# The overfull-expert branch of a two-layer MoE trunk moves from the first expert pair to the last, and a 1 MB weight piece loads earlier

## The chip, the cores and the metric

The kernel runs on one core of one Trainium2 chip. The metric is the device time of one execution in microseconds (us). A core has five engines, each with an instruction queue of its own: TensorE (PE: matmuls, with weight loads shown as PEld), VectorE (DVE), ScalarE (ACT), GpSimdE (POOL) and SyncE (SP), which here issues nearly all DMA transfers. Engines wait for one another on semaphores, each of which is a counter.

## The reference

Two layers, each of a token mixer and a mixture of experts, on 256 tokens of width 1024. The change touches the experts:

```python
for l in range(DEPTH):
    ...
    x = x + g1 * token_mix(h, positions, w_in[l], ...)
    h = rmsnorm(x, norm2_g[l]) * (1.0 + sc2) + sh2
    x = x + g2 * grouped_moe(h, w_router, router_bias, w_gate[l], w_up[l], w_down[l])
return rmsnorm(x, final_g)

def grouped_moe(h, w_router, router_bias, w_gate, w_up, w_down):
    ...                                   # 2 of 16 experts per token, weights in combine
    for e in range(N_EXPERTS):
        he = jax.nn.silu(t @ w_gate[e]) * (t @ w_up[e])
        y = y + combine[:, e:e + 1] * (he @ w_down[e])
```

## The kernel before

Each layer is a mixer and then `moe`. The router gives each of 16 experts its tokens, and a matmul with one-hot matrices (`gather`) copies up to CAP = 64 tokens of an expert into `xe` (in the trace `o`). The experts run in 8 pairs, `p` = 0 to 7: a gate product (`pair_mm(xs, 0, p)`), an up product (`pair_mm(xs, 1, p)`), `he` = silu(gate) times up on DVE, four transposes of `he` on PE, their copy `heT` on ACT, and the down product (`down`), whose result is scaled by the router's weights (`take_out`) and added to `xT` through a scatter matmul (`scatter`). In the last pair the down product goes in four pieces, each followed by a scatter, and then come the squares (`square_sum`) for the next norm. `warm` loads ACT's function table for the coming square root ahead of its use.

More than 64 tokens can pick one expert. `overflow()` handles them: all five engines load the largest count, `cmaxi`, into a register (L1141) and compare it with CAP at `tc.If` (L1144). On these inputs no engine takes the block: each jumps over its code and raises its semaphores by what the block would have raised them (EVENT_SEMAPHORE rows of L1144). Matmuls after the block write PSUM banks that the block's code uses too, so their waits count the semaphores past it. In the kernel before, the block stands between the gather and the first pair.

SP issues the weight loads in an order fixed when the program is built. `fetch` puts one into a buffer known by a tag; `issue` goes through the list `todo` and takes what has a free buffer: expert pieces ("moe", layer, pair, matrix, half) and the next mixer's sections ("sec", layer, name, half), of which "lat" comes first. Before the experts start, the first pair's weights and part of the second's are loaded: `early` and `late` put pieces into buffers that the mixer has done with. The last 1 MB of the second pair's up weights goes into buffer `n8`, by `latest`, after the block, because the block uses `n8` for its own tile `hT`.

The list of a tile scheduler, not the source alone, sets where instructions of different parts stand on an engine. The next mixer's first weight section is split into a rounded part and a rest: four CASTs on ACT and four TENSOR_TENSORs on DVE (helper line L409, reading `sec_lat_0A`). They stand, before the change, between the last squares of layer 0.

Of the kernel before, what the change touches and what calls it, by code (L numbers as in the profile page):

```python
# [50 lines left out]
HALF = SEC // 2  # L51
QUART = SEC // 4
# [103 lines left out]
def trunk(ctx: ExitStack, tc: tile.TileContext, x, pos, vec_in, msk_in, lat_in, wb, wq_in, wkv_in, ada_in, adat_in, crow_in, we,  # L156
# [10 lines left out]
    def nm(s):  # L167
        uid[0] += 1
        return f"{s}_{uid[0]}"

    def bank():
        return ps.tile([P, 512], F32, tag="bank", name=nm("bank"))
# [12 lines left out]
    free = set(size) - {"vm", "attn", "hA"}  # L185
# [3 lines left out]
    def load(o, src):  # L189
        tc.keep_in_program_order(nc.sync.dma_start(o, src))  # L190

    def fetch(key, tag, src, at=0, cuts=1):
        assert tag in free, (key, tag)
        free.discard(tag)
        n = src.shape[-1]
        t = wk.tile([P, size[tag]], F32, tag=tag, bufs=1, name=nm("_".join(map(str, key)) + tag))
        o = t if len(src.shape) == 2 else t.rearrange("p (q n) -> p q n", n=n)
        for c in range(cuts):
            c = slice(c * n // cuts, (c + 1) * n // cuts)
            load(o[..., c], src[..., c])  # L200
        held.setdefault(key, []).append((at, t, tag))
# [20 lines left out]
    def first_load(h):  # L222
        for q in (h, h + 1):
            for i in (1, 0):
                nc.sync.dma_start(first[i, h][:, (q - h) * QUART:(q - h + 1) * QUART], ada_in[i, q])
# [10 lines left out]
    def issue():  # L236
        while todo and not todo[0]:
            todo.pop(0)
        for n, part in enumerate(todo[:2]):
            while part:  # L240
                key = part[0]
                if key[0] == "sec":
                    tags = ("A0", "A1", "B0") if key[2] in ("lat", "qf") else ("A0", "A1")
                elif key[1] > layer[0] or n and todo[0] and (todo[0][0][0] == "moe" or todo[0][0][2] in ("lat", "qf")):
                    break
                else:
                    tags = ("B0", "B1", "C0", "C1", "x0", "x1") + (() if n and todo[0] else ("A0", "A1"))
                s = [t for t in tags if t in free and t not in blocked]
                if not s:
                    break  # L250
                part.pop(0)
                if key[0] == "sec":
                    _, l, name, h = key
                    fetch(key, s[0], lat_in[l, h] if name == "lat" else wb[l, SECTIONS.index(name), h],
                          cuts=4 if key == ("sec", 1, "lat", 0) else 1)
                    if key == ("sec", 0, "lat", 0):
                        first_load(2)
                else:
                    _, l, p, i, h = key
                    fetch(key[:4], s[0], we[l, p, i][:, h * HALF:(h + 1) * HALF], h * HALF,  # L260
                          cuts=(1 if p < E // 2 - 1 else 4 if (i, h) in ((1, 1), (2, 1)) else 2))
            if part and part[0][0] == "moe":
                break
        while atodo:
            s = [t for t in ("r0", "r1") if t in free]
            if not s:
                break
            key = atodo.pop(0)
            fetch(key, s[0], adat_in[key[1:]])
# [6 lines left out]
            at += size[t]  # L276

    def late(l):
        free.add("hA")
        fetch(("moe", l, 1, 1), "hA", we[l, 1, 1][:, HALF:HALF + QUART], HALF)  # L280

    def latest(l):
        at = HALF + QUART
        fetch(("moe", l, 1, 1), "n8", we[l, 1, 1][:, at:at + QUART], at)

    def take(*key):
        return held[key][0][1]
# [2 lines left out]
        free.update(tag for _, _, tag in held.pop(key))  # L290
        issue()

    again, used_up = {}, {}

    def spent(l, p, i, j):
        for e in list(held["moe", l, p, i]):
# [642 lines left out]
    def moe(l):  # L939
# [187 lines left out]
        def scatter(p, chunks=range(4)):  # L1127
            for i in chunks:
                b = bank()
                for q in range(2):  # L1130
                    j = 2 * i + q
                    for n in range(2):
                        mm(b[:, q * T:(q + 1) * T], yv[:, n, j * P:(j + 1) * P], St[p // 4][:, p % 4, :],
                           n == 0, n == 1)
                for q in range(2):
                    j = 2 * i + q
                    ve.scalar_tensor_tensor(xT[:, j, :], b[:, q * T:(q + 1) * T], g2[:, j:j + 1],  # L1137
                                            xT[:, j, :], op0=ALU.mult, op1=ALU.add)

        def overflow():  # L1140
            over = nc.values_load(cmaxi[0:1, 0:1], engines=[ENG.SP, ENG.Activation, ENG.DVE, ENG.PE, ENG.Pool],  # L1141
                                  min_val=0, max_val=T)
            room = [t2("room", [P, 512]) for _ in range(4)]
            with tc.If(over > CAP):  # L1144
                hT = solo("n8", [P, J, T])
                for t in range(NT):
                    for i in range(2):
                        b = bank()
                        for q in range(4):
                            for n, x in enumerate((hth, htl)):  # L1150
                                mm(b[:, q * P:(q + 1) * P], x[:, t, 4 * i + q, :], identr, n == 0, n == 1)
                        for q in range(4):
                            j = 4 * i + q
                            ve.tensor_scalar(hT[:, j, t * P:(t + 1) * P], b[:, q * P:(q + 1) * P],
                                             acol[:, j:j + 1], sh2[:, j:j + 1], op0=ALU.mult, op1=ALU.add)
                with tc.For_i(0, E // 2, 1) as p:
                    for q in range(2):
                        spill(l, p, q, hT, left[:, :, q::2], g2, room)
# [1 line left out]
        gather(oh, (0, 1), 2)  # L1160
        gather(oh, (2, 3))
        weights(0, oh)
        overflow()
        latest(l)
        for p in range(E // 2):
            xs = lambda j, q: xe[:, j, p % 2, 64 * q:64 * q + 64]
            bg = pair_mm(xs, 0, p)
            he = t2("he", [P, FJ, P])
            sg = t2("sg", [P, FJ, P])
            ac.activation(sg, bg.rearrange("s (j f) -> s j f", j=FJ), AF.Silu)  # L1170
            last = p == E // 2 - 1
            if last:
                scatter(p - 1)
            nxt = p + 1 if p % 2 and not last else None
            if nxt:
                oh = one_hot(nxt)
            bu = pair_mm(xs, 1, p)
            ve.tensor_tensor(he, bu.rearrange("s (j f) -> s j f", j=FJ), sg, ALU.mult)  # L1178
            if nxt:
                gather(oh)  # L1180
                weights(nxt, oh)
                build_scatter(nxt, oh)
            elif p and not last:
                scatter(p - 1, (0, 1))
            b = bank()
            for j in range(FJ):
                pe.transpose(b[:, j * P:(j + 1) * P], he[:, j, :], ident)  # L1187
            heT = t2("heT", [P, FJ, P])
            ac.copy(heT, b.rearrange("p (j s) -> p j s", j=FJ))  # L1189
            if p and not last:  # L1190
                scatter(p - 1, range(4) if nxt else (2, 3))
            wc = wcol[:, p:p + 1]
            def take_out(b, c, n):
                d = slice(c * 256, (c + n) * 256)
                s = slice(c % 2 * 256, (c % 2 + n) * 256)
                ac.activation(yv[:, 0, d], b[:, s], AF.Copy, scale=wc)  # L1196
                ve.scalar_tensor_tensor(yv[:, 1, d], b[:, s], wc, yv[:, 0, d], op0=ALU.mult, op1=ALU.subtract)  # L1197

            if last:
                warm(heT[:, 0, 0:1])  # L1200
            else:
                b0, b1 = bank(), bank()
                down(heT, p, b0, 0, 2)
            if p == 0:
                down(heT, p, b1, 2, 1)
                down(heT, p, b1, 3, 1)
                St = [solo(n, [P, 4, T], F32R) for n in ("vm", "attn")]
                yv = solo("r1", [P, 2, D], F32R)
                build_scatter(0, one_hot(0))
                take_out(b0, 0, 2)  # L1210
                take_out(b1, 2, 2)
            elif not last:
                take_out(b0, 0, 2)
                down(heT, p, b1, 2, 2)
                take_out(b1, 2, 2)
            else:
                for c in range(4):
                    b = bank()
                    down(heT, p, b, c, 1)
                    take_out(b, c, 1)  # L1220
                    if c:
                        scatter(p, (c - 1,))
# [89 lines left out]
```

## Time and profile before

| | |
|---|---|
| median of 3 runs | 987.47 us (983.97 to 988.82) |
| the profiled execution | 983.23 us |
| its span, first to last instruction | 981.4 us |
| mean granted TensorE clock | 0.963 of full |
| PE busy | 893.2 us, 91% of the span |
| DMA | 316.71 MB, mean 323 GB/s |

The profiled execution is 4.2 us under the median. Layer 0's experts take about 293 to 510 us of the span, layer 1's about 755 to 972 us; in these stretches PE works nearly without a break and the DMA queues are close to full. A matmul row's time is modelled, so a busy PE is not PE at its peak.

### The profile page before, as it was taken

The page shows a single profiled execution, that of the slowest core. Times are in us where ns is not written, and L with a number is a line of the kernel's source. Part 1 is how long each engine was busy: PE and PEld are TensorE (multiplying, and loading weights), DVE is VectorE, ACT ScalarE, POOL GpSimd, SP SyncE. Part 2 cuts the span into 40 slices and gives each one's busy share as a digit, 9 for nine tenths or more (in the row PEclk, how much of TensorE's full clock was granted, in tenths as well). Part 3 has the DMA queues.
Part 4 walks back from the last instruction along what each step waited for, and adds up shares of the span by engine and source line. Part 5 has one row for each costly group of instructions (what it writes and reads, how often), then busy time and mean ns, then how long its engine had stood idle before and what let it go on. Part 6 is the DMA issues. An engine that isn't in the chain of part 4 may idle for free. (4 is left out here: it accounts for less than half of the span.)

```text
span 981.4 us, 14762 instructions
## 1 busy us (share of the span) xinstructions
PE 893.2 (91%) x5958; PEld 635.6 (65%) x5958; DVE 524.3 (53%) x972; ACT 340.5 (35%) x632; POOL 51.9 (5%) x42
## 2 busy tenths in 40 slices
PE   5899999967969999999979999997895999999995
PEld 3688999957953535344349989997894353535333
DVE  4469898998540322222256968979854122322224
ACT  5465564524340212111146646554434111111103
POOL 0001100023000000000000020002300000000002
PEclk9899999998879999999999999999997999999998
DMA  9996665977659899999978626686585979999991
GB/s 362 430 378 225 234 224 217 380 307 315 253 210 381 344 384 430 434 427 429 422 299 329 271 91 248 253 326 250 224 348 200 398 306 433 429 429 433 426 386 43
DMA packets 35648, 316.71 MB, mean 323 GB/s; under 512 B 3952, under 2 KB 4208, under 8 KB 13808
## 3 DMA queue, kind: packets, MB, share of 16 engines
q1 hardware_dynamic: 35568, 315.64, 79.5%
q8 instruction: 50, 0.82, 0.3%
q14 instruction: 30, 0.25, 0.1%
HBM read 314.58 MB, written 1.05 MB: 322 GB/s over the span
## 5 line engine op out<-in xcount | busy, mean ns | idle before, releaser
L551 PE MATMUL bank<-hA,x 128*128 128x256 f32 x1312 | 242.8, 286 | 16.1 <-ACT x L409 8.8
L551 PEld LDWEIGHTS bank<-hA,x 128*128 128x128 f32 x1312 | 205.5, 192 | 20.3 <-DVE x L409 9.9
L551 PE MATMUL bank<-hB,x 128*128 128x256 f32 x656 | 184.7, 282 | 0.0
L551 PEld LDWEIGHTS bank<-hB,x 128*128 128x128 f32 x656 | 125.9, 192 | 0.2
L1178 DVE TENSOR_TENSOR he<-bank,sg 128x512 f32<-128x512 f32 x16 | 11.1, 692 | 141.8 <-PE bank L1112 113.4
L1137 DVE SCALAR_TENSOR_TENSOR xT<-bank,mod,xT 128x256 f32<-128x256 f32 x128 | 52.9, 478 | 58.1 <-PE bank L181 58.1
L1197 DVE SCALAR_TENSOR_TENSOR r<-bank,small,r 128x512 fp32r<-128x512 f32 (+1 forms) x36 | 24.7, 691 | 95.1 <-ACT r L1196 95.1
L1196 ACT ACTIVATE r<-bank,small 128x512 fp32r<-128x512 f32 (+1 forms) x36 | 22.8, 638 | 103.4 <-PE bank L1121 103.2
L1112 PE MATMUL bank<-moe_0B,o 128*64 128x512 f32 x192 | 47.6, 645 | 6.0 <-DVEq L1144 3.4
L1170 ACT ACTIVATE sg<-bank 128x512 f32<-128x512 f32 x16 | 9.6, 597 | 111.6 <-PE bank L1112 111.6
L1112 PE MATMUL bank<-moe_1x,o 128*64 128x512 f32 x192 | 43.4, 593 | 0.0
L1103 ACT ACTIVATE o<-bank,mod,acol 128x256 f32<-128x256 f32 x32 | 18.1, 564 | 58.5 <-DVE o L1105 55.0
L1189 ACT COPY heT<-bank 128x512 f32<-128x512 f32 x16 | 9.4, 588 | 83.4 <-PE bank L1187 83.4
L1112 PEld LDWEIGHTS bank<-moe_0B,o 128*64 128x64 f32 x192 | 15.2, 148 | 33.1 <-issue 32.6
L1112 PE MATMUL bank<-moe_1C,o 128*64 128x512 f32 x160 | 36.1, 592 | 0.0
L1105 DVE TENSOR_SCALAR o<-bank,acol,mod 128x256 f32<-128x256 f32 x32 | 17.4, 544 | 31.1 <-PE bank L181 28.2
L551 PE MATMUL bank<-o,x 128*128 128x256 f32 x192 | 28.1, 304 | 6.4 <-ACT x L409 3.4
L551 PE MATMUL bank<-attn,x 128*128 128x256 f32 x128 | 26.6, 300 | 6.4 <-DVE x L409 5.0
L1121 PE MATMUL bank<-moe_2C,heT 128*64 128x512 f32 (+1 forms) x160 | 29.2, 511 | 2.7 <-ACT heT L1189 2.7
L697 POOL TENSOR_TENSOR x<-ra,rbt 32x512 f32<-32x512 f32 x8 | 12.9, 1613 | 354.0 <-DVE rbt L693 353.5
L551 PEld LDWEIGHTS bank<-o,x 128*128 128x128 f32 x192 | 26.4, 212 | 7.2 <-ACT x L409 3.8
L1112 PEld LDWEIGHTS bank<-moe_1x,o 128*64 128x64 f32 x192 | 13.9, 137 | 26.2 <-issue 25.9
(298 smaller groups left out, 1719.6 us busy)
## 6 DMA issues: line engine op xcount, KB each, us to landing
moe_0B<-in_we SPq DMA_DIRECT2D x8, 2048.0 KB, 9.5
moe_1x<-in_we SPq DMA_DIRECT2D x8, 2048.0 KB, 13.0
moe_0A<-in_we SPq DMA_DIRECT2D x8, 2048.0 KB, 12.5
moe_1C<-in_we SPq DMA_DIRECT2D x6, 2048.0 KB, 12.3
moe_2C<-in_we SPq DMA_DIRECT2D x6, 2048.0 KB, 14.0
moe_1A<-in_we SPq DMA_DIRECT2D x6, 2048.0 KB, 18.1
moe_2A<-in_we SPq DMA_DIRECT2D x6, 2048.0 KB, 15.4
moe_2x<-in_we SPq DMA_DIRECT2D x6, 2048.0 KB, 20.1
```

The lines of the kernel that those rows point to most:

```text
L551: pe.matmul(o, a[:, k, :], b[:, k0 + k, :], start=first and k == 0 and q == 0, stop=last and k == 3 and q == 2)
L697: gp.tensor_tensor(qT[64:96, i::4, :], ra[q4], rbt[q4], ALU.add)
L1103: ac.activation(o, bq, AF.Identity, bias=sh2[:, j:j + 1], scale=acol[:, j:j + 1])
L1105: ve.tensor_scalar(o, bq, acol[:, j:j + 1], sh2[:, j:j + 1], op0=ALU.mult, op1=ALU.add)
L1112: pe.matmul(b[64 * q:64 * q + 64, :], x(j, q), w[:, o:o + 512], start=(j == 0), stop=(j == J - 1), tile_position=(0, 64 * q))
L1121: pe.matmul(b[64 * q:64 * q + 64].rearrange("p (c n) -> p c n", n=256)[:, c % 2:c % 2 + n], x[:, j, 64 * q:64 * q + 64], _ap(w[:, o:o + 25 ...
L1137: ve.scalar_tensor_tensor(xT[:, j, :], b[:, q * T:(q + 1) * T], g2[:, j:j + 1], xT[:, j, :], op0=ALU.mult, op1=ALU.add)
L1170: ac.activation(sg, bg.rearrange("s (j f) -> s j f", j=FJ), AF.Silu)
L1178: ve.tensor_tensor(he, bu.rearrange("s (j f) -> s j f", j=FJ), sg, ALU.mult)
L1189: ac.copy(heT, b.rearrange("p (j s) -> p j s", j=FJ))
L1196: ac.activation(yv[:, 0, d], b[:, s], AF.Copy, scale=wc)
L1197: ve.scalar_tensor_tensor(yv[:, 1, d], b[:, s], wc, yv[:, 0, d], op0=ALU.mult, op1=ALU.subtract)
```

## The change

It does four things in each of the two layers. `overflow()` leaves the place ahead of the first pair and stands in the last pair, behind the copy `heT` (and `warm` comes behind it in the source). `latest` is merged into `late`: the 1 MB piece in `n8` is issued at the mixer's end. A set `hold` keeps `issue` from issuing mixer sections, except the first half of "lat", from the last pair's gate product until the block is behind. Nothing is computed otherwise than before.

```diff
@@ -239,6 +239,8 @@
                 key = part[0]
+                if key[0] in hold and key[3:] and key[2:] != ("lat", 0):
+                    break
                 if key[0] == "sec":
@@ -276,12 +278,10 @@
     def late(l):
-        free.add("hA")
-        fetch(("moe", l, 1, 1), "hA", we[l, 1, 1][:, HALF:HALF + QUART], HALF)
-
-    def latest(l):
-        at = HALF + QUART
-        fetch(("moe", l, 1, 1), "n8", we[l, 1, 1][:, at:at + QUART], at)
+        for n, t in enumerate(("hA", "n8")):
+            at = HALF + n * QUART
+            free.add(t)
+            fetch(("moe", l, 1, 1), t, we[l, 1, 1][:, at:at + QUART], at)
@@ -290,7 +290,7 @@
-    again, used_up = {}, {}
+    again, used_up, hold = {}, {}, set()
@@ -1160,8 +1160,6 @@
         weights(0, oh)
-        overflow()
-        latest(l)
         for p in range(E // 2):
@@ -1170,6 +1168,7 @@
             if last:
+                hold.add("sec")
                 scatter(p - 1)
@@ -1187,6 +1186,10 @@
             ac.copy(heT, b.rearrange("p (j s) -> p j s", j=FJ))
+            if last:
+                overflow()
+                hold.clear()
+                issue()
             if p and not last:
```

Where this moves instructions shows in the built programs. On PE, at the start of layer 0's experts, the rows before are these (the first is the product `weights`, the last the first pair's gate product; the block's code is left out):

```order
L181 MATMUL bank_2663<-sr_2614,oh_2599 128x2 x8
L1141 TENSOR_LOAD cmaxi_2612
L1144 COMPARE_AND_BRANCH
...
L1144 UNCONDITIONAL_BRANCH
L1112 MATMUL bank_3482<-moe_0_0B_57_417,o_253_2618 64x512 x8
```

and of the changed kernel, at the same place and then in the last pair of layer 0 (L1186 are the transposes of `he`, L1121 is the down product):

```order
L181 MATMUL bank_2665<-sr_2616,oh_2601 128x2 x8
L1112 MATMUL bank_2676<-moe_0_0B_57_417,o_254_2620 64x512 x8
...
L1112 MATMUL bank_3676<-moe_7_1C_385_3530,o_254_2620 64x512 x8
L1186 MATMUL bank_3694<-vec,he_3645 128x128 x4
L1141 TENSOR_LOAD cmaxi_2614
L1144 COMPARE_AND_BRANCH
...
L1144 UNCONDITIONAL_BRANCH
L1121 MATMUL bank_4509<-moe_7_2C_389_3547,heT_3699 64x256 x8
```

The gate product now follows `weights` at once, and the load and the branch stand between the transposes and the first piece of the down product. That piece waits for DVE's and ACT's semaphores at counts (635 and 291) that neither reaches before it has passed the block (465 and 282 before it).

On ACT, in the last pair of layer 0, the rows before are these (L1189 is the copy `heT`, L386 `warm`, L1196 `take_out`, L390 the squares, L409 the casts of the next layer's first section, L396 the square root of the norm):

```order
L1189 COPY heT_4505<-bank_4500 128x512
L386 ACT_TABLE_LOAD
L386 ACTIVATE warm_4507<-heT_4505,epsb 128x1
L1196 ACTIVATE r_365_3575<-bank_4509,small_2256 128x256
...
L390 ACTIVATE sq_4592<-xT 128x512
L1196 ACTIVATE r_365_3575<-bank_4556,small_2256 128x256
L409 CAST x_528_4610<-sec_lat_0A_494_4415 128x512 x3
L390 ACTIVATE sq_4596<-xT 128x512
L409 CAST x_528_4610<-sec_lat_0A_494_4415 128x512
L396 ACTIVATE rstd_4622<-bank_4583,epsb 128x256
```

and of the changed kernel (L1188 is `heT`, L1199 `take_out`):

```order
L1188 COPY heT_3699<-bank_3694 128x512
L386 ACT_TABLE_LOAD
L386 ACTIVATE warm_4507<-heT_3699,epsb 128x1
L409 CAST x_528_4610<-sec_lat_0A_399_3609 128x512 x4
L1141 TENSOR_LOAD cmaxi_2614
L1144 COMPARE_AND_BRANCH
...
L1199 ACT_TABLE_LOAD
L1199 ACTIVATE r_270_2769<-bank_4509,small_2256 128x256
...
L396 ACT_TABLE_LOAD
L396 ACTIVATE rstd_4622<-bank_4583,epsb 128x256
```

The four casts have come ahead of the block, and two table loads are added behind it. DVE shows the same with the four subtractions that follow the casts:

```order
L1177 TENSOR_TENSOR he_3645<-bank_3676,sg_3646 128x512
L409 TENSOR_TENSOR x_528_4610<-sec_lat_0A_399_3609,x_528_4610 128x512 x4
L1141 TENSOR_LOAD cmaxi_2614
L1144 COMPARE_AND_BRANCH
```

Before, they stood among the last additions to `xT` behind the down product. In layer 1, which no mixer follows, no such casts or subtractions exist, and the block follows `warm` on ACT and `he` on DVE directly.

## Rows read from the trace of the kernel before

**Rows 1.** Waits of PE, 292 to 500 us: total us, times, longest

```profile
...
PE bank L1112 <- PEq L1144: 2.6, 1, 2.6
...
```

**Rows 2.** Timeline at the start of layer 0's experts: start us, us, engine, instruction, [idle before]

```profile
289.46 0.95 PE L181 MATMUL bank<-sr,oh 128*128 128x2 f32 x8
...
292.98 9.76 PE L1112 MATMUL bank<-moe_0B,o 128*64 128x512 f32 x32 [2.56 <-PEq L1144]
...
302.56 3.62 PE L1112 MATMUL bank<-moe_1x,o 128*64 128x512 f32 x16
...
305.99 3.61 PE L1112 MATMUL bank<-moe_1C,o 128*64 128x512 f32 x16
```

**Rows 3.** Timeline at the start of layer 1's experts

```profile
755.57 8.78 PE L1112 MATMUL bank<-moe_0B,o 128*64 128x512 f32 x32 [3.44 <-DVEq L1144]
...
764.16 3.63 PE L1112 MATMUL bank<-moe_1x,o 128*64 128x512 f32 x16
```

**Rows 4.** Register load and branch, L1141 and L1144, layer 0: duration ns, first and last start

```profile
L1141 PEldq TENSOR_LOAD <-cmaxi x1: 490/490/490, 288.3 to 288.3; - x1
L1141 DVEq TENSOR_LOAD <-cmaxi x1: 544/544/544, 290.5 to 290.5; - x1
...
L1144 PEldq COMPARE_BRANCH  x1: 3768/3768/3768, 288.9 to 288.9; - x1
...
L1144 DVEq EVENT_SEMAPHORE  x1: 21/21/21, 291.7 to 291.7; - x1
L1144 PEldq EVENT_SEMAPHORE  x1: 51/51/51, 292.7 to 292.7; - x1
```

**Rows 5.** The same of layer 1, DVE

```profile
L1141 DVEq TENSOR_LOAD <-cmaxi x1: 322/322/322, 752.2 to 752.2; - x1
...
L1144 DVEq EVENT_SEMAPHORE  x1: 21/21/21, 755.5 to 755.5; - x1
```

**Rows 6.** Busy time by stretch: PE, PEld, DVE, ACT, POOL, granted clock, DMA share, GB/s

```profile
284.00:286.00 2.00, 2.00 (x11) 2.00 (x10) 2.00 (x4) 0.00 (x0) 0.00 (x0) 0.50 0.00 0
293.00:295.00 2.00, 2.00 (x6) 0.81 (x8) 0.00 (x0) 0.00 (x0) 0.00 (x0) 0.50 0.57 131
```

**Rows 7.** Timeline in the last pair of layer 0

```profile
494.26 0.66 PE L1187 MATMUL bank<-vec,he 128*128 128x128 f32 x4 [0.86 <-DVE he L1178]
494.95 0.59 ACT L1189 COPY heT<-bank 128x512 f32<-128x512 f32 x1 [7.78 <-PE bank L1187]
495.56 1.28 ACT L386 ACT_TABLE_LOAD   x1
...
495.59 3.67 PE L1121 MATMUL bank<-moe_2C,heT 128*64 128x256 f32 x32 [0.68 <-ACT heT L1189]
496.85 0.29 ACT L386 ACTIVATE warm<-heT,epsb 128x1 f32<-128x1 f32 x1
...
505.98 1.65 ACT L409 CAST x<-sec_lat_0A 128x512 fp32r<-128x512 f32 x3
...
508.13 1.98 DVE L409 TENSOR_TENSOR x<-sec_lat_0A,x 128x512 fp32r<-128x512 f32 x3
```

**Rows 8.** Loads into `sec_lat_0A`: four issued 483 to 490 us; the last alone

```profile
DMA to landing us min/median/max: 8.2/10.8/11.9
...
L190 SPq DMA_DIRECT2D sec_lat_0A<-in_lat x1: 328/328/328, 489.6 to 489.6; - x1
...
DMA to landing us min/median/max: 8.2/8.2/8.2
```

**Rows 9.** Timeline in the last pair of layer 1, and the final norm

```profile
955.90 0.66 PE L1187 MATMUL bank<-vec,he 128*128 128x128 f32 x4 [0.86 <-DVE he L1178]
...
957.23 3.67 PE L1121 MATMUL bank<-moe_2C,heT 128*64 128x256 f32 x32 [0.67 <-ACT heT L1189]
...
970.44 0.49 ACT L1271 ACTIVATE hB<-xT,vec 128x256 f32<-128x256 f32 x1
972.01 0.47 ACT L396 ACTIVATE rstd<-bank,epsb 128x256 f32<-128x256 f32 x1 [1.08 <-PE bank L181]
```

## The prediction

> **What bounds the kernel now.** I read the waits of PE first, over the stretch of layer 0's experts. Of all the time that PE stood idle there, one wait is longer than a microsecond: 2.6 us ahead of the first gate product, released by PE's own queue at L1144, the branch [rows 1]. No wait on a DMA is among them, so the experts are bound by PE, and what PE loses or gains at their ends moves the end of the kernel by as much. Then I read the timeline at both places of the branch. `weights` ends at 289.46 + 0.95 = 290.41 us and the gate product starts at 292.98: 2.57 us lost [rows 2]. In layer 1 the gate product's row shows 3.44 us idle before it [rows 3].
>
> There is a second loss behind the first. At full rate half a product takes 305.99 - 302.56 = 3.43 us, so a whole one 6.86; the first gate product takes 302.56 - 292.98 = 9.58 in layer 0 [rows 2] and 764.16 - 755.57 = 8.59 in layer 1 [rows 3]: 2.72 and 1.73 us more. [...]
>
> **What the branch costs each engine.** PE begins its register load at 288.3, compares at 288.9, and raises its semaphore at 292.7: 4.4 us, of which 3.77 are the compare-and-branch itself [rows 4]. DVE needs 290.5 to 291.7 = 1.2 us in layer 0 [rows 4] and 752.2 to 755.5 = 3.3 in layer 1 [rows 5]. A wait ahead of the register load holds it back: DVE's starts only at 290.5, when the matmuls of `weights`, for which its last copies wait, have ended at 290.41 [rows 2, 4]; the count itself was ready for PE at 288.3.
>
> [...]
>
> **What the change removes.** Both losses at the start of each layer's experts: 2.57 + 2.72 = 5.29 us in layer 0 and 3.44 + 1.73 = 5.17 in layer 1, together **10.46 us**. The gate product then follows `weights` without a gap. PE had been busy for some time at the half clock before it rose [rows 6], and with no pause I expect it to stay up.
>
> **The moved 1 MB load.** It is issued behind `hA` at the mixer's end. Between 284 and 286 us the DMA engines move nothing [rows 6], so it lands in time that nobody uses; it is free, and SP's queue ahead of the reloads becomes shorter. If that cover were gone it would push the reloads back by 1 MB, which PE, with no DMA wait anywhere in this stretch [rows 1], would hardly see. `hold` costs nothing either: the next load behind the block waits for a buffer that the down product frees.
>
> **What the change adds in layer 1's last pair.** The transposes wait for `he` until 955.90, and the register load stands behind them. 4.4 us later, at 960.3, PE raises its semaphore, and 0.28 us later (292.7 to 292.98 before) the down product starts: 960.6 in place of 957.23 [rows 4, 9], **3.35 us**. DVE's branch starts with `he`, some 0.7 us earlier, and is over before PE's even at 3.3 us. The bound from below is 0, if PE's branch took DVE's 1.2 us here; I take PE's own, seen alike in both layers.
>
> **In layer 0's last pair** more comes ahead of the branch: on ACT `heT` (to 495.54), the table load (to 496.84), `warm` (to 497.14) and four casts. The last of the four loads lands at 489.6 + 8.2 = 497.8 [rows 8], before the fourth cast would start, so they run at their pace: three in 1.65 us, so 0.53 apart [rows 7]. DVE subtracts behind each cast, three in 1.98 us, so 0.65 apart [rows 7]: the first starts behind the first cast, some 0.6 us after 497.14, at 497.7, the fourth at 499.7, done at 500.4. DVE's register load starts with the fourth, and the semaphore is raised 1.2 to 3.3 us later, at 500.9 to 503.0. The down product waits for it and starts at 501.0 to 503.1 in place of 495.59 [rows 7]: 5.4 to 7.5 us. No row says which of DVE's two durations applies, so I take the middle, **6.45 us**. PE's own branch would be over at about 494.3 + 4.4 = 498.7 [rows 4, 7]. Ahead of the change these casts and subtractions lay beside PE's last work and cost nothing; taking them from there gives nothing back.
>
> **The clock after these pauses.** [...] I take the mean of the two losses seen, 2.2 us in each layer: **4.45 us** (3.46 to 5.44). The down pieces and scatters behind it are PE's work in a row, so it counts in full.
>
> **Table loads.** Two more per layer, 1.28 us each [rows 7]. The first lies beside the first down piece. The second stands between the last ACT instruction and the square root: 970.44 + 0.49 + 1.28 = 972.21 against 972.01 [rows 9], **0.2 us** in layer 1; I give the same place in layer 0 nothing.
>
> **Sum.** -10.46 + 3.35 + 6.45 + 4.45 + 0.2 = **+4.0 us**; with the bounds of DVE's branch and of the clock +1.9 to +6.0. By layer: layer 0 loses about 3.4 and layer 1 about 0.6. The profiled execution took 983.23 us, so one like it would take 987.2; the median of the runs is 4.2 us higher, and with it I get **991.5 us**. The change moves a short pause to a place where more waits for it.
>
> **Rivals.**
> - *The fetch is slower under load* (slower). In layer 0 the branch comes at 494.9, while weights still stream. If PE's branch lasted as long as those loads take to land, 8.2 to 11.9 us [rows 8], the down product would start at 503.4 to 507.1, and the sum is +5.4 to +9.1 us. For it: the first branch ran while the DMA engines were idle [rows 6]. Against: PE's code comes in through the whole stretch of full DMA queues, and no wait for it shows there but the branch [rows 1]. It decides from 8.0 us on.
> - *The gain at the start is half* (slower). If the clock falls at the start anyway, its 4.45 us stay lost: +8.4 us. Against: no pause is left there.
> - *The branch is cheap in the last pair* (not slower). If PE needs only what DVE needed in layer 0, it is through before `heT` is there, layer 1 loses neither the 3.35 nor the 2.2 us, and layer 0 only 5.4: -2.6 us, or -4.8 if the clock holds in layer 0 too. Against: 3.77 us of PE in a row [rows 4]. It decides where PE's branch takes less than 1.2 us.
>
> **Chances.** The forecast 0.58, the slow fetch 0.18, the half gain 0.09, the cheap branch 0.15. A measurement of this kernel tells about 0.5% (4.9 us) from no change. Above +4.9 us lie a third of the forecast's cases and nearly all of the two slower rivals: 0.42. Below -4.9 us lies little of the cheap branch: 0.08. Within: 0.50. The forecast's own range is 989.4 to 993.5 us; for 8 in 10 I go to the cheap branch below and to the slow fetch above, and add some for runs that spread over 5 us: 984.5 to 997.
>
> **What would show it.** Right: the gate product starts within 0.3 us of `weights` and takes about 6.9 us in both layers; PE then waits, ahead of the first L1121 matmul of the last pair, some 6 us longer than before in layer 0, released by DVE's queue, and 3.4 us longer in layer 1, released by PE's own; the granted clock behind both is 0.50. Wrong: a last pair whose branch costs PE under 1.5 us, a clock that stays up behind it, a DMA wait among PE's waits, or casts that start later than 498 us of the old count.

## The result, and the profile after

| | before | after |
|---|---|---|
| median | 983.85 us (979.0 to 988.8, 20 runs) | 989.39 us (986.9 to 992.1, 20 runs) |
| the profiled execution | 983.23 us | 986.93 us |
| its span | 981.4 us | 985.2 us |
| mean granted clock | 0.963 | 0.961 |

The ratio of after to before is 1.0057, with a 95% interval of 1.0042 to 1.0071: 0.6% slower, or 4.1 to 7.0 us. Of two profiled executions, the one after took 3.70 us more; it is the fastest of its 20 runs, 2.5 us under their median, so that this pair shows less than the medians do. One run of the version with the chunk at its old place took 1548.07 us at a granted clock of 0.554 and is left out of the times below.

**The starts.** PE's timeline of the changed kernel at the start of layer 0's experts (`weights`, gate, up), and of layer 1's:

```profile
288.97 0.95 PE L181 MATMUL bank<-sr,oh 128*128 128x2 f32 x8
289.85 7.09 PE L1112 MATMUL bank<-moe_0B,o 128*64 128x512 f32 x32
296.77 3.60 PE L1112 MATMUL bank<-moe_1x,o 128*64 128x512 f32 x16
...
755.59 0.95 PE L181 MATMUL bank<-sr,oh 128*128 128x2 f32 x8
756.47 7.09 PE L1112 MATMUL bank<-moe_0B,o 128*64 128x512 f32 x32
763.39 1.89 PE L1112 MATMUL bank<-moe_1x,o 128*64 128x512 f32 x8
```

The gate product has no idle time in its row, and from its start to that of the up product it is 6.92 us. In layer 0 the up product starts at 296.77 against 302.56 [rows 2], 5.79 us earlier; 0.49 of that was there at `weights`, so the gain is 5.30. In layer 1 `weights` ends at 756.54 against 755.57 - 3.44 = 752.13 [rows 3], 4.41 us later, and the up product starts 0.77 us earlier: 5.18.

The 1 MB piece is issued at 276.06 us, before at 292.80. The stretch in which the DMA engines moved nothing [rows 6] is now full (columns as there):

```profile
284.00:286.00 2.00, 2.00 (x12) 2.00 (x11) 2.00 (x4) 0.00 (x0) 0.00 (x0) 0.50 0.94 397
```

**The last pair of layer 0.** First the waits of PE, 288 to 500 us (total, times, longest), then the timeline of the last pair:

```profile
PE bank L1121 <- DVEq L1144: 8.1, 1, 8.1
```

```profile
488.49 0.66 PE L1186 MATMUL bank<-vec,he 128*128 128x128 f32 x4 [0.86 <-DVE he L1177]
497.29 6.06 PE L1121 MATMUL bank<-moe_2C,heT 128*64 128x256 f32 x32 [8.14 <-DVEq L1144]
...
491.28 2.16 ACT L409 CAST x<-sec_lat_0A 128x512 fp32r<-128x512 f32 x4
...
491.92 2.50 DVE L409 TENSOR_TENSOR x<-sec_lat_0A,x 128x512 fp32r<-128x512 f32 x4 [3.48 <-ACT x L409]
```

The start's gain arrives whole: the transposes begin 494.26 - 488.49 = 5.77 us earlier than in [rows 7]. Then the first down piece waits 8.14 us where it waited 0.68, a stall of 7.46 us, and takes 6.06 us for what took 3.67. The row names DVE's queue as what released it, and DVE's four subtractions stand ahead of its branch. The branch rows of this place (duration ns, first and last start):

```profile
L1144 PEldq COMPARE_BRANCH  x1: 6122/6122/6122, 489.1 to 489.1; - x1
...
L1144 DVEq COMPARE_BRANCH  x1: 72/72/72, 494.1 to 494.1; - x1
L1144 PEldq EVENT_SEMAPHORE  x1: 51/51/51, 495.3 to 495.3; - x1
L1144 DVEq EVENT_SEMAPHORE  x1: 21/21/21, 497.0 to 497.0; - x1
```

PE is through at 495.3, DVE at 497.0, and PE starts 0.3 us later. But PE's compare-and-branch took 6122 ns, not the 3768 of [rows 4].

**The clock.** Windows of the changed kernel (columns as in [rows 6]):

```profile
290.00:293.00 3.00, 3.00 (x16) 1.00 (x16) 0.27 (x2) 1.60 (x2) 0.00 (x0) 1.00 0.35 74
497.00:499.00 2.00, 1.71 (x8) 1.14 (x10) 0.00 (x0) 0.00 (x0) 0.00 (x0) 0.50 0.01 4
501.00:503.00 2.00, 2.00 (x16) 1.25 (x12) 0.48 (x1) 0.47 (x1) 0.00 (x0) 0.71 0.00 0
```

At the experts' start the clock is full (1.00). Behind the stall it is 0.50, and full again from about 502 us. Before the change it was 0.50 behind the pause at layer 0's start [rows 6], and so for most of the first 2 us behind layer 1's pause of 3.44 us, ahead of which it was full:

```profile
750.00:752.20 2.20, 2.13 (x20) 2.05 (x18) 1.37 (x5) 1.43 (x4) 0.00 (x0) 1.00 0.05 11
...
755.50:757.50 2.00, 1.93 (x6) 0.84 (x8) 0.00 (x0) 0.00 (x0) 0.00 (x0) 0.57 0.51 86
```

With no pause ahead of it the first gate product takes its 6.92 us at 1.00, so the 2.72 and 1.73 us more of [rows 2, 3] go with the clock. The first products of the next mixer run at 0.50 in both kernels, before from 513.74 to about 516.9 us and after from 516.96 to about 522.6.

**The last pair of layer 1, and the end.**

```profile
955.12 0.66 PE L1186 MATMUL bank<-vec,he 128*128 128x128 f32 x4 [0.86 <-DVE he L1177]
959.70 5.26 PE L1121 MATMUL bank<-moe_2C,heT 128*64 128x256 f32 x32 [3.93 <-PEq L1144]
...
972.16 3.04 PE L181 MATMUL bank<-sq,one 128*128 128x256 f32 x12
...
974.43 1.28 ACT L396 ACT_TABLE_LOAD   x1
975.73 0.47 ACT L396 ACTIVATE rstd<-bank,epsb 128x256 f32<-128x256 f32 x1
```

From the transposes to the down product it is 4.58 us against 1.33 [rows 9]: a stall of 3.25 us on PE's own branch, and 1.59 us more for the piece, in which the clock is 0.51 (961 to 963 us).

### The profile page after: what moved, and what is told of

Read it like the earlier page. It is cut to its first block, busy times and chain, and to the rows that moved or that the text cites. A ratio compares the mean times of both kernels' runs of the same rounds, so it can differ in the third digit from the quotient of the medians.

```text
span 985.2 us, 14780 instructions
## 1 busy us (share of the span) xinstructions
PE 895.0 (91%) x5958; PEld 637.5 (65%) x5958; DVE 524.3 (53%) x972; ACT 345.8 (35%) x636; POOL 52.0 (5%) x42
## 5 line engine op out<-in xcount | busy, mean ns | idle before, releaser
L1199 ACT ACTIVATE r<-bank,small 128x512 fp32r<-128x512 f32 (+1 forms) x36 | 22.8, 639 | 113.1 <-PE bank L1121 112.9
L1121 PE MATMUL bank<-moe_2C,heT 128*64 128x512 f32 (+1 forms) x160 | 33.2, 570 | 13.4 <-DVEq L1144 8.1
L1112 PE MATMUL bank<-moe_0B,o 128*64 128x512 f32 x192 | 43.2, 595 | 0.0
L1188 ACT COPY heT<-bank 128x512 f32<-128x512 f32 x16 | 9.4, 587 | 83.4 <-PE bank L1186 83.4
L1121 PEld LDWEIGHTS bank<-moe_2C,heT 128*64 128x64 f32 x160 | 13.5, 161 | 29.5 <-issue 26.8
```

Source lines behind the costliest of these rows:

```text
L1112: pe.matmul(b[64 * q:64 * q + 64, :], x(j, q), w[:, o:o + 512], start=(j == 0), stop=(j == J - 1), tile_position=(0, 64 * q))
L1121: pe.matmul(b[64 * q:64 * q + 64].rearrange("p (c n) -> p c n", n=256)[:, c % 2:c % 2 + n], x[:, j, 64 * q:64 * q + 64], _ap(w[:, o:o + 25 ...
```

## The experiments

Each is set beside the kernel before on the same chip. Each profiled execution has an offset of its own: the product `weights` of layer 0 starts anywhere from 288.97 to 293.10 us. So I compare distances within one execution, and medians or ratios for the whole. A ratio is not the quotient of the two medians beside it, and the two differ by nearly 0.2% at most; its interval is what a verdict rests on. Where a version goes on from another, its diff is against that one.

### The casts behind the block

Against the changed kernel:

```diff
-                if key[0] in hold and key[3:] and key[2:] != ("lat", 0):
+                if key[0] in hold:
...
+            last = p == E // 2 - 1
+            if p == E // 2 - 2:
+                hold.add("sec")
             bg = pair_mm(xs, 0, p)
...
-            last = p == E // 2 - 1
             if last:
-                hold.add("sec")
                 scatter(p - 1)
```

> The changed kernel with the loads of the next mixer's input held back until the block has been passed, so that the eight casts and subtractions (L409) come behind the block on ScalarE and VectorE. Theory (the stall of 7.5 us in layer 0 is VectorE's, which comes to its branch late behind the casts): TensorE's wait ahead of the last down product in layer 0 falls to what its own branch takes, 3.3 to 3.7 us, and the time falls by some 4 us against the changed kernel, to about 985 us, less whatever the later casts cost in the mixer (0 to 2 us). Rival (instruction fetch under the DMA load makes TensorE's own branch 6.1 us long there): the wait falls only to about 5.7 us and the time by about 2 us, to 987 us. Layer 1 has no such casts and stays as it is, with its wait of 3.9 us on TensorE's own branch.

Measured: 982.86 us, the kernel before on that chip 985.74; ratio 0.9971 (0.9952 to 0.9990). In layer 0:

```profile
L1144 PEldq COMPARE_BRANCH  x1: 3902/3902/3902, 491.4 to 491.4; - x1
...
L1144 DVEq EVENT_SEMAPHORE  x1: 21/21/21, 493.8 to 493.8; - x1
```

```profile
490.81 0.66 PE L1187 MATMUL bank<-vec,he 128*128 128x128 f32 x4 [0.86 <-DVE he L1178]
495.73 6.57 PE L1121 MATMUL bank<-moe_2C,heT 128*64 128x256 f32 x32 [4.26 <-PEq L1144]
```

The wait is 4.26 us, 3.6 of it stall, and PE's own branch releases it: the theory's 3.3 to 3.7. So the 7.5 us were DVE's lateness. The rival isn't refuted by it, though: PE's branch took 3.9 us here, but the loads were moved as well, and between 491 and 494 us the DMA engines were 0.23 busy. The clock fell as in the changed kernel (0.50 from 497 to 501 us, 6.57 us for the piece). From the transposes to the next mixer's first product it is 515.92 - 490.81 = 25.11 us against 516.96 - 488.49 = 28.47, 3.4 us less, which is about the theory's 4 less the later casts. The medians say more, 5.9 us against the version with the chunk at its old place (below; the same as the changed kernel in all else, on this chip); the rest is not placed.

### Loads beside the branch

To the version above, in the last pair ahead of the up product:

```diff
+            if last:
+                for t in [t for t in ("A0", "A1", "B0", "B1") if t in free and t not in blocked][:2]:
+                    load(wk.tile([P, size[t]], F32, tag=t, bufs=1, name=nm("extra"))[:, :2688], we[l, p, 0][:, :2688])
             bu = pair_mm(xs, 1, p)
```

> The version with the mixer's loads held, plus two loads of 1.3 MB in each layer that nothing reads, issued ahead of the last up product, so that the DMA engines are busy while TensorE takes its branch; nothing else is changed. Theory (the branch is long because its target's instructions are fetched beside data transfers): TensorE's branch grows from 3.9 and 3.5 us to about 6 us in both layers, as in the changed kernel in layer 0, the wait ahead of the last down product to 6 to 6.5 us, and the time by 3 to 6 us. Rival (6.1 us in the changed kernel had to do with the casts or with where the code lies): the branch stays at 3.5 to 3.9 us, and the time grows by 0 to 1 us.

Measured: 989.44 us, before 984.65; ratio 1.0047 (1.0024 to 1.0069). The branch rows of layer 0, then of layer 1:

```profile
L1144 DVEq COMPARE_BRANCH  x1: 72/72/72, 490.2 to 490.2; - x1
L1144 PEldq COMPARE_BRANCH  x1: 5882/5882/5882, 490.9 to 490.9; - x1
L1144 DVEq EVENT_SEMAPHORE  x1: 21/21/21, 495.5 to 495.5; - x1
...
L1144 PEldq COMPARE_BRANCH  x1: 5999/5999/5999, 955.5 to 955.5; - x1
```

and its windows over the two branches (the share of the DMA engines is the last number but one):

```profile
490.90:496.80 5.90, 0.03 (x1) 0.00 (x0) 0.00 (x0) 2.16 (x3) 0.00 (x0) 0.75 0.82 341
955.50:961.60 6.10, 0.23 (x3) 0.00 (x0) 0.00 (x0) 3.45 (x4) 0.00 (x0) 0.71 0.84 350
```

With nothing but loads added, the branch grew from 3902 and 3499 ns to 5882 and 5999, also in layer 1, where no casts were ever in the way; DVE's went from 3.1 to 5.3 us. The waits ahead of the down products are 6.25 and 6.19 us. The theory stands for the branch, which is longer beside data transfers (shares of 0.82 and 0.84 here, 0.53 and 0.04 without the extra loads); the last section shows in the changed kernel which part of it is. The two waits grew by 1.99 and 2.50 us, 4.5 together. The time grew by more, from 0.9971 to 1.0047 of before, some 7 us on two chips; SP, behind whose branch the mixer's own loads stand, raises its last semaphore of layer 0's block at 497.8 us here, at 491.8 without the extra loads, and that part is not taken apart.

### The block left out

```diff
             if last:
-                overflow()
                 hold.clear()
                 issue()
```

> The changed kernel with the overfull-expert block left out of both layers; on these inputs no expert is overfull, so that the output doesn't change, but that part of the computation is missing. Theory (the gain of 10.5 us at the start of the experts is real and carried to the end, and the loss is all at the last pair: stalls of 7.5 and 3.3 us, and the clock that falls in them): no wait ahead of either last down product, no fall of the clock there, and the time is that of before less 10.5 us, less about 1 us at the end of each layer: 971 to 974 us. Rival (part of the gain at the start is given back on the way, for example by the weights that are loaded faster or slower): 976 us or more.

Measured: 975.01 us, before 985.74; ratio 0.9874 (0.9856 to 0.9892). In absolute time that lies between the theory and the rival. Beside its own kernel before it is 10.7 us under by the medians and 10.6 to 14.2 by the ratio, and the start gain forecast was 10.46, so that gain is carried to the end. This version keeps `hold`, and from the transposes to the next mixer's first product it takes 510.10 - 490.62 = 19.48 us, as before the change (513.74 - 494.26): `hold` costs nothing. The last pair of layer 0, and the row of its last scatter:

```profile
491.95 3.67 PE L1121 MATMUL bank<-moe_2C,heT 128*64 128x256 f32 x32 [0.67 <-ACT heT L1188]
...
502.50 0.38 PE L181 MATMUL bank<-attn,r 128*128 128x256 f32 x1 [0.98 <-ACT r L1198]
```

Without the stall the piece takes 3.67 us, against 6.06 behind it: the clock's loss comes from the stall. PE pauses later, 3.42 us ahead of the mixer's first product at 510.10, and here the clock stays full behind it, where before the change a pause of 3.41 us at this place was followed by 0.50:

```profile
510.00:514.00 4.00, 3.90 (x34) 3.90 (x35) 4.00 (x11) 3.01 (x9) 0.00 (x0) 1.00 0.90 375
```

The 0.98 us ahead of the last scatter, which the expectation took for gone, is there, in both layers; why, is told below.

### The chunk at its old place

```diff
     def late(l):
...
+    def latest(l):
+        at = HALF + QUART
+        free.add("n8")
+        fetch(("moe", l, 1, 1), "n8", we[l, 1, 1][:, at:at + QUART], at)
...
         weights(0, oh)
+        latest(l)
         for p in range(E // 2):
```

> The changed kernel with the second early weight chunk of 1 MB issued where it was before, behind the weights of the first pairs, instead of at the mixer's end. Theory (the chunk has a large margin, and the start gain is the block's alone): no change against the changed kernel, within 0.5 us. Rival (with the block gone from there the first up product would wait for the chunk): a wait of the up product of the first pair in each layer, and 1 to 6 us more.

Measured: 988.71 us, before 985.74; ratio 1.0031 (1.0013 to 1.0049), which overlaps the changed kernel's interval. Its gate product takes 299.82 - 292.90 = 6.92 us as in the changed kernel, and PE waits for no load there. The chunk's move makes no difference that these times can tell, and PE's rows show none; the half microsecond of the theory is finer than the intervals.

### The second layer alone

```diff
         weights(0, oh)
+        if not l:
+            overflow()
+            latest(l)
...
-            if last:
+            if last and l:
                 overflow()
```

(The chunk and `hold` go with it.)

> The change in the second layer alone: in layer 0 the block and the second early chunk stand where they stood before. Theory (each layer pays and gains for itself): at the start of the experts layer 1 gains 5.2 us, and at its last pair it loses 3.3 us of wait, 1.6 us of clock and 0.5 us for the table load, and gets 0.95 us back behind the last take_out: 0.5 to 1 us under the kernel before, which is no difference that can be measured, and 4 to 5 us under the changed kernel. Rival (the gains and losses of one layer depend on the other, through the clock or the weights' loads): outside 3 us under to 2 us over the kernel before.

Measured: 984.75 us, before 984.65; ratio 0.9999 (0.9976 to 1.0022). The first down pieces of the two layers' last pairs (its lines are numbered 4 higher):

```profile
499.06 3.67 PE L1125 MATMUL bank<-moe_2C,heT 128*64 128x256 f32 x32 [0.68 <-ACT heT L1196]
...
957.77 5.20 PE L1125 MATMUL bank<-moe_2C,heT 128*64 128x256 f32 x32 [3.65 <-PEq L1148]
```

Layer 1 gains at one end what it loses at the other; the loss of the changed kernel is layer 0's. The changed kernel's own rows agree: from `weights` of layer 0 to the end of `weights` of layer 1 it takes 756.54 - 288.97 = 467.57 us against 752.13 - 289.46 = 462.67, 4.9 more (1.2 of it in the mixer between, of which more below), and from there to the end of the span 0.6 less.

### The block behind the gate product

To the version with the casts held: `overflow()` and the release of `hold` move up.

```diff
             if last:
+                overflow()
+                hold.clear()
+                issue()
                 scatter(p - 1)
...
-            if last:
-                overflow()
-                hold.clear()
-                issue()
```

> The changed kernel with the block moved from behind the transposes of the last pair to behind its gate product (and the mixer's loads held as in the other run). Theory (the price of the block is the time from when TensorE's queue comes to the branch until it is past it, less the matmuls still running then): the 32 gate matmuls let TensorE's queue run ahead by about 2 us, so the wait is 1.5 to 2 us in each layer instead of 7.5 and 3.3, little clock is lost, and the time is 976 to 981 us, under both kernels. Rival (fetch under the full DMA load takes 6.1 us or more in layer 0): a wait of about 4 us there, and 981 to 985 us. Rival (any stop ahead of the last down product costs the clock, wherever it is): about 4 us more than the theory says.

Measured: 989.12 us, before 985.74; ratio 1.0023 (1.0008 to 1.0037). The forecast of 976 to 981 us failed. In layer 0:

```profile
482.26 2.83 PE L181 MATMUL bank<-attn,r 128*128 128x256 f32 x16 [2.50 <-PEq L1144]
...
500.82 1.11 PE L1190 MATMUL bank<-vec,he 128*128 128x128 f32 x4 [7.21 <-DVE he L1181]
...
499.48 0.69 DVE L409 TENSOR_TENSOR x<-sec_lat_0A,x 128x512 fp32r<-128x512 f32 x1 [0.73 <-ACT x L409]
500.08 0.69 DVE L1181 TENSOR_TENSOR he<-bank,sg 128x512 f32<-128x512 f32 x1
```

The branch costs PE 2.5 us, and, against the theory, the clock too (columns as in [rows 6]):

```profile
484.00:486.00 2.00, 2.00 (x10) 1.16 (x9) 2.00 (x6) 0.00 (x0) 0.00 (x0) 0.50 1.00 410
```

With the release ahead of `he`, moreover, the scheduler put the casts and subtractions ahead of `he` too, and these wait for loads that SP issues only at 492 us, when it is past its own branch (479.0 to 491.8 us). `he` is 7 us late: the same DVE queue as in the changed kernel, one step further up. In layer 1, without casts, PE waits 2.35 us at the block, the clock stays at 1.00 behind it, and nothing more is lost at the down product.

### The block behind the up product

To the version with the casts held:

```diff
             ve.tensor_tensor(he, bu.rearrange("s (j f) -> s j f", j=FJ), sg, ALU.mult)
+            if last:
+                overflow()
...
             if last:
-                overflow()
                 hold.clear()
                 issue()
```

> The version with the mixer's loads held, with the block moved ahead by one step: behind the last pair's up product and the multiplication that makes `he`, ahead of the transposes. Theory (TensorE's queue comes to the branch while the up product's matmuls still run, 3.8 us ahead of the array as it did behind the gate product, and its branch takes 6.0 us beside the weight loads): TensorE waits 2.2 to 2.5 us there, of which 0.9 us is the wait for `he` that is there anyway, so that each layer pays some 1.5 us instead of the 4.3 and 3.9 us; with a clock that falls little in so short a wait the time is 3 to 6 us under the version with the loads held, and 5 to 9 us under the kernel before. Rival (a branch is waited for until the array is empty, so the place doesn't matter): no change against the version with the loads held. Rival (the clock falls in the shorter wait as well): 2 to 3 us under the version with the loads held.

Measured: 979.35 us, before 984.65; ratio 0.9940 (0.9919 to 0.9961). It is faster than the kernel before, by 5.3 us of median, inside the 5 to 9 expected. In layer 0:

```profile
L1144 PEldq COMPARE_BRANCH  x1: 5542/5542/5542, 484.2 to 484.2; - x1
L1144 DVEq COMPARE_BRANCH  x1: 72/72/72, 488.8 to 488.8; - x1
L1144 PEldq EVENT_SEMAPHORE  x1: 51/51/51, 489.8 to 489.8; - x1
L1144 DVEq EVENT_SEMAPHORE  x1: 21/21/21, 491.7 to 491.7; - x1
```

```profile
484.45 3.60 PE L1112 MATMUL bank<-moe_1C,o 128*64 128x512 f32 x16
...
491.85 0.80 PE L1189 MATMUL bank<-vec,he 128*128 128x128 f32 x4 [3.79 <-DVEq L1144]
493.32 6.46 PE L1121 MATMUL bank<-moe_2C,heT 128*64 128x256 f32 x32 [0.68 <-ACT heT L1191]
```

PE's branch starts at 484.2, while the up product's matmuls run to 484.45 + 3.60 = 488.05, so most of it lies beside work. The wait is not the 2.2 to 2.5 us expected but 3.79, and DVE's: its branch starts with `he` and ends at 491.7, and the transposes, which stand behind the block, count DVE's semaphore past it. The clock fell here too (0.50 from 495 to 498 us and from 954 to 956 us), as the second rival had it: the time came in where it was expected, but in each layer with a longer wait and a loss of clock.

### The block behind the gate product, in layer 1 alone

To the version above:

```diff
             if last:
+                if l:
+                    overflow()
                 scatter(p - 1)
...
-            if last:
+            if last and not l:
                 overflow()
```

> The version with the block behind the last up product, with one more step in layer 1 alone: there the block stands behind the last pair's gate product. Theory (behind the up product the transposes wait until VectorE is past its own branch, which it enters only when `he` is made, so that 3.8 us are waited for instead of TensorE's own 2.3; behind the gate product VectorE is past it early, and a wait of 2.3 us there costs no clock): layer 1 pays 2.3 us in place of 2.9 us of added wait and 1.5 us of clock, and the time is 1.5 to 2.5 us under that version. Rival (the transposes wait on TensorE's own branch in both places): within 0.5 us of that version.

> The version with the block behind the last up product in both layers once more, on the chip of the run beside it, so that the two can be compared: 0.992 to 0.996 of the kernel before, as in its first run.

Measured on one chip: this 977.45 us, the version above 980.18, before 983.80; ratios to before 0.9918 (0.9890 to 0.9945) and 0.9954 (0.9936 to 0.9972). In layer 1:

```profile
943.35 2.12 PE L181 MATMUL bank<-attn,r 128*128 128x256 f32 x16 [2.26 <-PEq L1144]
...
953.35 0.66 PE L1191 MATMUL bank<-vec,he 128*128 128x128 f32 x4 [0.86 <-DVE he L1180]
954.68 3.67 PE L1121 MATMUL bank<-moe_2C,heT 128*64 128x256 f32 x32 [0.68 <-ACT heT L1193]
```

```profile
944.00:948.00 4.00, 4.00 (x25) 2.18 (x25) 3.23 (x8) 0.00 (x0) 0.00 (x0) 1.00 0.99 397
```

The wait is 2.26 us on PE's own branch, the clock stays at 1.00 behind it, and the down piece takes 3.67 us. The medians differ by 2.7 us, a little over the 1.5 to 2.5 expected, but the two intervals overlap. The stages show it better: from layer 1's gate product to the end of the span it is 978.1 - 752.7 = 225.4 us against 977.3 - 749.6 = 227.7, 2.3 us less. The version above came out at 0.9954, as its repeat was expected to.

## Why the prediction was right, and where not

Forecast 991.5 us with a range of 984.5 to 997, measured 989.39. That the two are only 2.1 us apart is in part luck, because two errors work against each other. The base was 3.6 us too high: the sum was put on a median of 3 runs, 987.47, and 20 runs have 983.85. The change itself was 1.5 us too small: +4.0 us against 989.39 - 983.85 = +5.5, and the ratio's interval is 4.1 to 7.0 us. The profiled pair, with +3.70, looks closer, but its second execution is the fastest of 20. The forecast gave 0.50 to a change within 0.5% and 0.42 to one above it; the interval of 0.4 to 0.7% holds that bound. Term by term:

- **What the change removes: right.** 5.30 + 5.18 us against 5.29 + 5.17. It is carried to the last pair, and with the block left out all of it shows in the time.
- **The moved load costs nothing: right**, by the run with the chunk at its old place; it fills the stretch that stood empty. **`hold`: right**, by the version without the block.
- **Layer 1's stall: right.** 3.25 us against 3.35, on PE's own branch (3739 ns).
- **Layer 0's stall: right in mechanism, too small in size.** 7.46 us against 6.45. The casts and subtractions ran as forecast: they ended 494.42 - 488.49 = 5.93 us behind the start of the transposes, against 500.4 - 494.26 = 6.14. The term that was off is DVE's register load and branch: 3.5 us (493.5 to 497.0), where I took the middle of 1.2 and 3.3. Both of these were real durations; instruction packets start inside the longer one and none inside the shorter (last section). With the casts out of the way the stall was 3.6 us.
- **The clock after the pauses: right.** 2.39 + 1.59 = 3.98 us against 4.45, at a clock of 0.50 and 0.51 behind the two stalls.
- **The mixer between: not in the sum.** From its first product to the end of `weights` it takes 239.58 us against 238.39, 1.2 more. The longer stretch at 0.50 at its first products is not the reason: that loss is made up by the first product of `qr`, which comes 568.43 - 516.96 = 51.47 us behind the first product, before 565.35 - 513.74 = 51.61. Nearly all of the 1.2 us comes at the end, in the gather, which takes 756.54 - 749.27 = 7.27 us against 752.13 - 745.98 = 6.15; the clock is 0.50 in it to about 754.7 us, before to about 749.0. That the change brings this is not shown: from the mixer's first product to layer 1's gate product, one kernel, the block behind the up product, took 237.1 us in one profiled execution and 235.8 in the other.
- **Table loads:** 0.13 us in layer 0 and 975.73 - 975.20 = 0.53 in layer 1, against 0 and 0.2.
- **A gain that I missed.** Before, PE waited 0.98 us in each layer for the last `take_out`, which stood behind a square on ACT; in layer 0:

```profile
506.14 0.38 PE L181 MATMUL bank<-attn,r 128*128 128x256 f32 x1 [0.98 <-ACT r L1196]
```

After, `take_out` runs at once and the wait is gone in both layers, some -0.95 us each. It is gone in each last pair that has the block in it, in layer 1 too, where there are no casts, and is there in each that has not (both layers without the block; layer 0 with the change in the second layer alone). So it is the scheduler's order of `take_out` and the squares that comes with the block, not the casts, and I had not looked at that order.

The sum as measured: -10.48 + 7.46 + 3.25 + 3.98 + 1.2 + 0.66 - 1.9 = +4.2 us, less the 0.49 of offset ahead of the first experts: +3.7, as the profiled executions differ. That the forecast sum is so near is luck as well: what it had too small or left out (1.0 of stall, 1.2 of mixer, 0.5 of table loads) is made up by what it had too large or missed (0.5 of clock, 1.9 behind `take_out`). The other 1.8 us that the medians have are in no trace kept here.

**The rivals.** The slow fetch was there in layer 0 (6122 ns for 3768), but PE's branch ended 1.7 us before DVE's, so it cost nothing; it did not reach the 8 us from which it would decide. What was held against it, that PE's code comes in beside full queues without a wait (9 packets of kind instruction on q8 from 292 to 500 us before, and no wait of PE put down to them), does not carry over to the jump, which took 6122 ns at a share of 0.86. Where the casts are out of DVE's way the branch does set the wait, as the extra loads showed (6.25 and 6.19 us). The half gain did not happen: the clock is 1.00 at the start. The cheap branch did not happen either, in the last pair ahead of the down product; some of it can be had where PE's queue comes to the branch while long matmuls run (a branch of 5972 ns and a wait of 2.26 us behind layer 1's gate product).

## What to carry to other kernels

The block that no engine took here still cost the engines their jumps (3.5 to 6.1 us on PE, 0.6 to 5.4 on DVE) and made them wait for one another: price such a block per engine, from when that engine's queue reaches it, and look at what the scheduler has put ahead of it there. Put it where the engine that bounds the kernel has microseconds of matmuls queued ahead, and where the other engines are past it before anything behind it needs them. The same block cost +0.6% in the changed kernel and gave -0.5 to -0.8% in the best versions here, which differ from it in the block's place and in when the next mixer's loads are released.

## What the runs showed of the hardware

The duration of PE's compare-and-branch went with the share of DMA work beside it. At shares of 0.04 it took 3739 ns (changed kernel, layer 1) and 3499 (casts held, layer 1); at 0.53 3902 (casts held, layer 0); at 0.70 and 0.72 5542 and 5637 (behind the up product); at 0.82 and 0.84 5882 and 5999 (extra loads); at 0.86 6122 (changed kernel, layer 0); at 1.03 and 1.04 5972, 6028 and 6052 (behind the gate product).

The trace shows which part of it grows. PE's branch in layer 0 of the changed kernel runs from 489.1 to 495.2 us. These are the packets that the profile lists as instruction, from 489.1 to 492.8 us, and then from 492.8 to 493.9 (queue, kind: packets, MB, share of the 16 engines):

```profile
q14 instruction: 1, 0.01, 0.5%
...
q8 instruction: 1, 0.02, 5.6%
```

In each of the four branches of PE in the kernel before and the changed kernel one such 16 KB packet of q8 starts, and PE is past the branch 1.3 to 1.4 us after it has landed; that q8 brings PE's instructions is read from this. The packet itself takes 1.0 to 1.5 us, beside loads and without them. What grows is the time until it starts, counted from the branch's start: 1.0 us in both layers before (shares of 0.05 and 0.04) and 1.4 in layer 1 of the changed kernel (0.04), but 3.8 in its layer 0 (0.86).

DVE's branch, from compare to semaphore, took 2.9 us in layer 1 before and in both layers of the changed kernel, 2.8 to 3.1 with the casts held, 5.3 with the extra loads in both layers, and 5.4 behind the gate product in layer 1. But it took 0.6 us behind the gate product in layer 0 (474.3 to 474.9), beside full queues (a share of 1.02), and in layer 0 before the change (291.1 to 291.7). In the last of these no instruction packet starts between compare and semaphore, and in each of the three of 2.9 us one or two of 8 KB on q14 do; why there were none is not shown. SP's took longest: from its compare at 479.6 us to its first semaphore at 489.0 and its last at 491.8 in the version with the casts held.

The length of a pause does not decide alone whether the clock falls. Pauses of 2.26 and 2.35 us behind layer 1's last gate product, and one of 3.42 ahead of the mixer in the version without the block, left it at 1.00. One of 2.50 us behind layer 0's last gate product, with the clock at 1.00 from 475.9 to 482.0 us ahead of it, was followed by 0.50. In the last pairs, waits of 3.65 to 8.33 us were followed by a first down piece of 5.12 to 6.57 us in place of 3.67, and by a clock of 0.50 where it was read. What else decides was not tried. So the clock that the block behind layer 1's gate product saves is seen in two executions, and layer 0 shows that it is not sure.
